# Gate and norm products in three split parts, a new order of the key and value groups, and a new order of the first transfers, in a two-layer decoder trunk

## The chip, the cores and the metric

The kernel is one program for one core of a Trainium2 chip. The metric is the device time of one execution in microseconds (us), as the median of several runs; smaller is better. TensorE (PE in the rows) multiplies, VectorE (DVE), ScalarE (ACT) and GpSimd (POOL) work on elements, SyncE (SP) only starts transfers. ACT and POOL start transfers too, from their own streams of instructions.

## The reference

512 positions of width 1024 pass through two layers. The first is a gated linear recurrence, the second is attention over three groups of dilated windows, and each is followed by a SwiGLU block:

```
h = h + recurrent_mixer(rms_norm(h))      # layer 1
h = h + swiglu(rms_norm(h))
k, v = shared_kv(h)                       # 3 groups x 2 heads of keys and values
h = h + dilated_attention_mixer(rms_norm(h), k, v)    # 3 groups x 8 heads of queries
h = h + swiglu(rms_norm(h))
```

The part that the change touches most is the recurrent mixer:

```
y, x = split(h @ w_in)                    # 1024 -> 2 x 1024
xc = causal_depthwise_conv(x, 4 taps) + b
r, i = sigmoid(xc @ w_a + b_a), sigmoid(xc @ w_x + b_x)     # 8 blocks of 128 x 128
log_a = -8 * r * softplus(-lambda);  a = exp(log_a)
u = sqrt(1 - exp(2 log_a)) * (i * xc)
hr = scan(a, u)                           # h_t = a_t h_(t-1) + u_t
out = (gelu(y) * hr) @ w_out
```

## The kernel before, in words

Everything lies transposed on the chip: 128 features on the partitions, 512 positions in a row, so h is eight tiles of 128x512. A wide product is made of 128x128 weight tiles against 128x512 tiles of activations. Almost all products run in three parts (`mm3`, L146 to L148): weight and activation are each split into a high part of type float32r and the float32r rest (`wh`, `wl`, `xh`, `xl`), and high x high, high x low and low x high are added up in PSUM. Two sorts of product do not run so: the two gates of the recurrence (L388, L389), whose weights `gw` and activations `xc` are plain float32, and the row of norm factors that `norm_rows` (L260 to L265) spreads over all partitions with a matrix of ones (L263).

Weights stream in as pieces of 128x1024 through the class `Stream`: `_load` (L85) asks for a piece, as a rule on SP's queue; two raw pieces (`wr`) are held at a time. `_split` makes the parts: `wh` is a cast on ACT (L100); `wl` is a difference on DVE (L107), or, for pieces marked "dma", a negated copy on ACT (L103) onto which a transfer from POOL's queue adds the original (L104). The first two pieces come in three cuts each (256, 256 and 512 columns), their first cuts on ACT's queue.

The recurrence works by eight blocks of 128 features. `x_block` takes a block out of PSUM and multiplies by the norm row `rb` (`xp`, L377), then runs the four taps of the convolution: the first on ACT (L380), three on DVE (L382), which give `xc`. `x_gates` multiplies `xc` by the two gate weights, two blocks at a time, with sigmoids and a tanh on ACT (L395 to L398) behind. `decays` has the exponentials and square roots on ACT, `recur` the scan on DVE. These steps stand between the blocks of `w_in` (`in_block`), which are 24 matmuls each.

Keys and values (`project`, `done_kv`) run over three groups in the order 0, 1, 2. The values of group 1 are moved between partitions by 16 small transfers on POOL's queue (L755). Queries follow. In the attention itself (`attend`) PE goes through 32 units of scores (`scores`), transposes of the softmax (`turned`, L876) and value products (`values`); between them it is given filling: the projection of later queries (`project_q`, L710 to L712) and the first half of the output projection. Query heads are turned by PE (L789) into a PSUM bank "X" of which there is one, and copied out by ACT (L791). What is due later is put in a list by tick (`at`), which `tick` works off.

The order on each engine comes from a scheduler that follows the order of the program, apart from what stands in `tc.high_priority()` and what `behind` holds back.

## Time and profile before

| | us |
|---|---|
| median of 3 runs | 1215.19 (1214.24 to 1215.32) |
| the profiled execution | 1216.08 |
| its span on the chip | 1214.3 |
| PE busy in it | 1203.3 |
| DVE busy | 659.4 |
| ACT busy | 519.0 |
| POOL busy | 160.7 |

A row of the timeline gives the start and the length of one instruction, or of several alike in a row (xN), and in brackets how long its engine stood idle before and what it waited for. Lengths of matmuls overlap, since they are pipelined: what one costs is read from start to start. A plain float32 matmul leaves two records in the trace.

### The profile page before, as it was taken

To read this page: it belongs to the slowest core of one execution; us is meant where nothing else is said; L and a number is where in the kernel's file an instruction comes from. 1 tells how busy PE (TensorE), PEld (TensorE's weight loads), DVE (VectorE), ACT (ScalarE), POOL (GpSimd) and SP (SyncE) were. 2 spreads that over 40 slices of the span, in tenths; PEclk is the share of its full clock that TensorE was granted. 3 is DMA by queue.
4 is the path that set the end of the run, shared out by engine and by line. 5 is a ranking of instruction groups with operands and counts; after the bars stand their busy time and mean duration, and the time that the engine had idled before them with its cause. 6 is when DMAs were issued, how large, how long until landed. Compare 5 with 4: busy or idle time off the path is not lost.

```text
span 1214.3 us, 14690 instructions
## 1 busy us (share of the span) xinstructions
PE 1203.3 (99%) x5627; PEld 994.8 (82%) x5627; DVE 659.4 (54%) x1232; ACT 519.0 (43%) x751; POOL 160.7 (13%) x163
## 2 busy tenths in 40 slices
PE   9999999999999999999999999999999999999998
PEld 6778888888888888888788888898888888888887
DVE  8787675455454333377555667856545455542221
ACT  6795433323232222265555778655323223222110
POOL 0100001011110000010411344350011011110000
PEclk9999999999999999999999999999999999999999
DMA  7543332332223333323978688535223323233331
GB/s 247 137 104 104 113 109 93 104 97 95 92 99 100 95 96 96 100 97 95 221 173 181 157 177 203 130 71 139 87 93 99 104 90 101 89 98 113 114 116 43
DMA packets 42053, 141.81 MB, mean 117 GB/s; under 512 B 5248, under 2 KB 6144, under 8 KB 41984
## 3 DMA queue, kind: packets, MB, share of 16 engines
q1 hardware_dynamic: 33552, 113.97, 29.6%
q0 software_dynamic: 7280, 25.69, 12.0%
q10 hardware_dynamic: 1152, 1.23, 0.4%
q8 instruction: 44, 0.72, 0.2%
q14 instruction: 25, 0.20, 0.0%
HBM read 137.72 MB, written 2.10 MB: 115 GB/s over the span
## 4 chain that ended last, share of the span: by engine, by line
PE 92%; DVE 2%; DMA 2%; ACT 2%; issue 1%; POOL 1%; ACTq 0%; DVEq 0%; POOLq 0%
PE ps L147 26%; PE ps L148 25%; PE ps L146 25%; PE ps L710 4%; PE ps L711 4%; PE ps L712 4%; DMA wl<-in_w_q 2%; PE ps L789 1%; PE ps L876 1%; PE ps L388 1%; PE ps L389 1%; DVE ql L232 0%; ACT wl L103 0%; PE ps L248 0%; DVE sqc L647 0%
## 5 line engine op out<-in xcount | busy, mean ns | idle before, releaser
L100 ACT CAST wh<-wr 128x1024 fp32r<-128x1024 f32 (+3 forms) x216 | 219.4, 1016 | 480.0 <-PE ps L147 438.3
L146 PE MATMUL ps<-xh,wh 128*128 128x512 f32 x896 | 353.0, 394 | 0.2 <-ACT xh L226 0.2
L147 PE MATMUL ps<-xl,wh 128*128 128x512 f32 x896 | 349.2, 390 | 0.2 <-DVE xl L232 0.2
L148 PE MATMUL ps<-xh,wl 128*128 128x512 f32 x896 | 349.0, 389 | 0.0
L107 DVE TENSOR_TENSOR wl<-wr,wh 128x1024 fp32r<-128x1024 f32 (+2 forms) x169 | 241.0, 1427 | 147.2 <-ACT wh L100 147.1
L146 PEld LDWEIGHTS ps<-xh,wh 128*128 128x128 f32 x896 | 168.4, 188 | 37.0 <-issue 1.2
L147 PEld LDWEIGHTS ps<-xl,wh 128*128 128x128 f32 x896 | 168.3, 188 | 36.7 <-issue 1.7
L148 PEld LDWEIGHTS ps<-xh,wl 128*128 128x128 f32 x896 | 168.2, 188 | 34.8
L148 PE MATMUL ps<-gh,wl 128*128 128x512 f32 x352 | 136.9, 389 | 0.0
L147 PE MATMUL ps<-gl,wh 128*128 128x512 f32 x352 | 136.9, 389 | 0.0
L146 PE MATMUL ps<-gh,wh 128*128 128x512 f32 x352 | 136.9, 389 | 0.0
L493 POOL TENSOR_TENSOR u<-u,g 128x512 f32<-128x512 f32 x44 | 58.8, 1335 | 503.4 <-ACT wh L100 354.2
L492 DVE TENSOR_TENSOR u<-ps,rb 128x512 f32<-128x512 f32 x44 | 30.4, 691 | 135.6 <-PE ps L148 135.6
L710 PE MATMUL ps<-wh,xh 128*128 128x512 f32 x224 | 91.4, 408 | 0.0
L711 PE MATMUL ps<-wl,xh 128*128 128x512 f32 x224 | 87.8, 392 | 2.4 <-DMA wl<-in_w_q 2.4
L712 PE MATMUL ps<-wh,xl 128*128 128x512 f32 x224 | 87.7, 392 | 0.0
L148 PEld LDWEIGHTS ps<-gh,wl 128*128 128x128 f32 x352 | 66.1, 188 | 13.8
L146 PEld LDWEIGHTS ps<-gh,wh 128*128 128x128 f32 x352 | 66.1, 188 | 13.7
L147 PEld LDWEIGHTS ps<-gl,wh 128*128 128x128 f32 x352 | 66.1, 188 | 13.5
L490 DVE TENSOR_TENSOR g<-ps,rb 128x512 f32<-128x512 f32 x44 | 30.4, 691 | 63.7 <-PE ps L148 63.6
L103 ACT ACTIVATE wl<-wr 128x1024 fp32r<-128x1024 f32 x47 | 49.7, 1058 | 24.2 <-PE ps L711 24.1
L231 ACT CAST gh<-u 128x512 fp32r<-128x512 f32 x44 | 27.4, 622 | 60.8 <-POOL u L493 60.8
(214 smaller groups left out, 1459.0 us busy)
## 6 DMA issues: line engine op xcount, KB each, us to landing
wr<-in_f_in SPq DMA_DIRECT2D x88, 512.0 KB, 3.5
wr<-in_f_out SPq DMA_DIRECT2D x32, 512.0 KB, 3.6
wr<-in_w_q SPq DMA_DIRECT2D x32, 512.0 KB, 7.1
wl<-in_w_q POOLq DMA_DIRECT2D x32, 512.0 KB, 7.6
wr<-in_w_in SPq DMA_DIRECT2D x14, 512.0 KB, 3.9
wr<-in_f_out SPq DMA_DIRECT2D x16, 384.0 KB, 3.1
wr<-in_w_kv SPq DMA_DIRECT2D x12, 512.0 KB, 3.4
wr<-in_a_out SPq DMA_DIRECT2D x8, 512.0 KB, 3.4
```

The source lines that it names most:

```text
L100: nc.scalar.copy(hi[:, c], r[:, c])
L103: nc.scalar.mul(lo[:, c], r[:, c], -1.0)
L107: a = eng.tensor_tensor(lo[:, c], r[:, c], hi[:, c].bitcast(F32), ALU.subtract)
L146: PE.matmul(ps, wh, xh, start=first, stop=False)
L147: PE.matmul(ps, wh, xl, start=False, stop=False)
L148: PE.matmul(ps, wl, xh, start=False, stop=last)
L490: V.tensor_tensor(g, pair[0], rb, ALU.mult)
L492: V.tensor_tensor(u, pair[1], rb, ALU.mult)
L493: G.tensor_tensor(u, u, g, ALU.mult)
L710: PE.matmul(ps[t], xh[k][:, r], wh[:, c], start=k == 0, stop=False)
L711: PE.matmul(ps[t], xh[k][:, r], wl[:, c], start=False, stop=False)
L712: PE.matmul(ps[t], xl[k][:, r], wh[:, c], start=False, stop=k == 7)
```

## The change

- **Gates.** Gate weights are split like the others (`gwh`, `gwl`), from a raw piece that is cast and negated on ACT and added onto by a transfer of POOL's. `xc` is split by `x_parts` (high part by a cast on ACT, low part by a difference on DVE), and the gates run as `mm3`. The first tap of blocks 4 to 7 goes to POOL.
- **Norm rows.** `norm_rows` makes a high and a low diagonal (eight DVE operations where there were four) and multiplies both by ones in float32r.
- **Keys and values.** The groups come in the order 0, 2, 1 (the first, the third and the second), and their weights too.
- **Attention.** A unit has one place for filling where it had two, and the turns of the later queries (`kv` = 1) lie two ticks apart where they lay one apart.
- **Start.** The first tile of x is the first transfer of SP; the parameters go to ACT's queue. The second piece of weights comes by SP alone, its first cast waits for the first `xh`, two of nine warm-up matmuls go, and the first two weight blocks alternate by two feature tiles.

The diff, cut to its core:

```diff
@@ Stream._load, Stream._split
+                itertools.zip_longest(self._cuts(i, w), self.queues[i] if i < self.cut else (), fillvalue=self.nc.sync)]
...
+                a = nc.scalar.copy(hi[:, c], r[:, c])
+                if i in self.cast:
+                    behind(self.tc, a, self.cast.pop(i))
@@ the start
-    p_kv = add_pieces([A["w_kv"][i] for i in range(12)])
+    p_kv = add_pieces([A["w_kv"][i] for g in (0, 2, 1) for i in range(4 * g, 4 * g + 4)])
...
-        load_a, load_b, load_c, *splits = ws.start(2, nc.scalar)
-        nc.sync.dma_start(par, A["par"])
-        run(load_a)
+        load_a, load_b, load_c, *splits = ws.start(2, (nc.scalar,), ())
+        nc.scalar.dma_start(par, A["par"])
+        run(load_a[:1])
         for k in range(KB):
             nc.sync.dma_start(h[k], A["x"][k])
-            run({1: load_b, 3: load_c}.get(k, ()))
+            run({0: load_a[1:], 1: load_b, 3: load_c}.get(k, ()))
+        G.tensor_copy(ones_r, ones)
@@ norm_rows
-                a = V.tensor_scalar(dg[:, 128 * n:128 * n + 128], ident, r[:, n:n + 1], None, ALU.mult)
+                c = slice(128 * n, 128 * n + 128)
+                V.tensor_scalar(dh[:, c], ident, r[:, n:n + 1], None, ALU.mult)
+                a = V.scalar_tensor_tensor(dl[:, c], ident, r[:, n:n + 1], dh[:, c].bitcast(F32),
+                                           ALU.mult, ALU.subtract)
...
-            PE.matmul(ps, ones, dg, start=True, stop=True)
+            PE.matmul(ps, ones_r, dh, start=True, stop=False)
+            PE.matmul(ps, ones_r, dl, start=False, stop=True)
@@ the recurrence
-            for _ in range(9):
+            for _ in range(7):
...
+                    else:
+                        ws.cast[1] = a
...
-            for k in range(KB):
-                c = slice(128 * k, 128 * k + 128)
+            for k2 in range(0, KB, 2):
                 for ps, (wh, wl) in zip(first, parts):
-                    mm3(ps, (wh[:, c], wl[:, c]), (xh[k], xl[k]), k == 0, k == KB - 1)
-            gw = [lp.tile([128, 1024], F32, name=f"gw{i}", bufs=1) for i in range(2)]
-            for g in range(2):
-                nc.sync.dma_start(gw[g], A["gates"][g])
+                    for k in (k2, k2 + 1):
+                        c = slice(128 * k, 128 * k + 128)
+                        mm3(ps, (wh[:, c], wl[:, c]), (xh[k], xl[k]), k == 0, k == KB - 1)
...
+            for g in range(2):
+                raw = lp.tile([128, 1024], F32, name="gwr", tag="rate", bufs=4)
+                nc.sync.dma_start(raw, A["gates"][g])
+                S.copy(gwh[g], raw)
+                S.mul(gwl[g], raw, -1.0)
+                nc.gpsimd.dma_start(gwl[g], A["gates"][g], accum_op=ALU.add)
@@ x_block, x_parts, x_gates
-                S.activation(xc, xp[:, 0:T], AF.Identity, bias=gain(C_CB, b), scale=cw[0])
+                if b < 4:
+                    S.activation(xc, xp[:, 0:T], AF.Identity, bias=gain(C_CB, b), scale=cw[0])
+                else:
+                    G.tensor_scalar(xc, xp[:, 0:T], cw[0], gain(C_CB, b), ALU.mult, ALU.add)
...
+            def x_parts(b, xc):
+                parts = [lp.tile([128, T], F32R, name=n) for n in ("xch", "xcl")]
+                halve(xc, *parts)
+                return b, xc, parts
...
-                PE.matmul(pr, gw[0][:, c], xc, start=True, stop=True)
-                PE.matmul(pi, gw[1][:, c], xc, start=True, stop=True)
+                for g, ps in enumerate((pr, pi)):
+                    mm3(ps, (gwh[g][:, c], gwl[g][:, c]), parts, True, True)
...
+                if i in (4, 5, 7, 8):
+                    xs[:2] = [x_parts(*x) for x in xs[:2]]
@@ attention
-            at(lag + j, lambda t=t: turn(t, kn[t]))
+            at(lag + apart * j, lambda t=t: turn(t, kn[t]))
...
-    for g in range(3):
+    for j, g in enumerate((0, 2, 1)):
...
-                    normed(st, 4, 0, turn, {3: 11, 4: 7}.get(j, 8), tiles)
+                    normed(st, 4, 0, turn, {3: 11, 4: 7}.get(j, 8), tiles, 1 + kv)
...
             if u >= LAG:
                 turned(*units[u - LAG])
-            yield u + 0.4
             if u < 32:
                 scores(*units[u])
             yield u + 1.0
...
-        if k % 2:
-            tick()
+        tick()
```

How instructions move is shown at three places. The first is DVE ahead of the first group of gates (blocks 0 and 1), from the `xp` of blocks 2 and 3 on. Before:

```order
L377 TENSOR_TENSOR xp_423<-ps_234,rb_314 128x4x4x32
L377 TENSOR_TENSOR xp_431<-ps_282,rb_314 128x4x4x32
L382 SCALAR_TENSOR_TENSOR xc_426<-xp_423,par_74,xc_426 128x512
L382 SCALAR_TENSOR_TENSOR xc_434<-xp_431,par_74,xc_434 128x512
L382 SCALAR_TENSOR_TENSOR xc_426<-xp_423,par_74,xc_426 128x512
L382 SCALAR_TENSOR_TENSOR xc_434<-xp_431,par_74,xc_434 128x512
L107 TENSOR_TENSOR wl7_456<-wr7_448,wh7_455 128x1024
```

and now, where `xcl_456` and `xcl_460` are the low parts of blocks 0 and 1, and `xc_450` is block 4, whose first tap is POOL's:

```order
L397 TENSOR_TENSOR xp_439<-ps_278,rb_316 128x4x4x32
L237 TENSOR_TENSOR xcl_456<-xc_418,xch_455 128x512
L405 SCALAR_TENSOR_TENSOR xc_434<-xp_431,par_74,xc_434 128x512
L405 SCALAR_TENSOR_TENSOR xc_442<-xp_439,par_74,xc_442 128x512
L405 SCALAR_TENSOR_TENSOR xc_434<-xp_431,par_74,xc_434 128x512
L110 TENSOR_TENSOR wl7_472<-wr7_464,wh7_471 128x1024
L405 SCALAR_TENSOR_TENSOR xc_434<-xp_431,par_74,xc_434 128x512
L405 SCALAR_TENSOR_TENSOR xc_442<-xp_439,par_74,xc_442 128x512
L397 TENSOR_TENSOR xp_447<-ps_324,rb_316 128x4x4x32
L405 SCALAR_TENSOR_TENSOR xc_442<-xp_439,par_74,xc_442 128x512
L405 SCALAR_TENSOR_TENSOR xc_450<-xp_447,par_74,xc_450 128x512
L237 TENSOR_TENSOR xcl_460<-xc_426,xch_459 128x512
```

The low part of block 1 stands behind seven taps, the `wl` of a weight piece and an `xp`, though its own `xc_426` is finished before the first of these rows.

The second place is POOL's queue where the values are moved. Before, transfers of query weights (`wl` from `in_w_q`) stand ahead of, between and behind the moves, of which this is a piece:

```order
L755 DMA vh_3697<-ph 64x2x128
L755 DMA vh_3696<-ph 64x2x128
L104 DMA wl_4486<-in_w_q 128x1024
L755 DMA vh_3697<-ph 64x2x128
L755 DMA vl_3698<-pl 64x2x128
L755 DMA vl_3699<-pl 64x2x128
```

and now, at the end of the moves:

```order
L787 DMA vl_3785<-pl 64x2x128
L787 DMA vl_3784<-pl 64x2x128
L787 DMA vl_3785<-pl 64x2x128
L107 DMA wl_4342<-in_w_q 128x1024
L107 DMA wl_4401<-in_w_q 128x1024
```

All 16 moves now stand ahead of the first transfer of query weights.

The third place is PE in the attention, between two turns of query heads (`ident,kn`). Before, with value products (`ph`, `pl`) and transposes of the softmax (`ident,pr`) between them:

```order
L789 MATMUL ps<-ident,kn 128x128 x4
L146 MATMUL ps<-ph,vh_3696 128x256
L147 MATMUL ps<-pl,vh_3696 128x256
L148 MATMUL ps<-ph,vl_3698 128x256
L146 MATMUL ps<-ph,vh_3696 128x128
L147 MATMUL ps<-pl,vh_3696 128x128
L148 MATMUL ps<-ph,vl_3698 128x128
L146 MATMUL ps<-ph,vh_3696 128x128
L147 MATMUL ps<-pl,vh_3696 128x128
L148 MATMUL ps<-ph,vl_3698 128x128
L876 MATMUL ps<-ident,pr 128x128 x3
L789 MATMUL ps<-ident,kn 128x128 x4
```

and now, at two turns of another unit, with filling between them (`wh`, `wl` against `xh`, `xl`):

```order
L821 MATMUL ps<-ident,kn 128x128 x4
L741 MATMUL ps<-wh_5566,xh 128x512
L742 MATMUL ps<-wl_5567,xh 128x512
L743 MATMUL ps<-wh_5566,xl 128x512
L741 MATMUL ps<-wh_5566,xh 128x512
L742 MATMUL ps<-wl_5567,xh 128x512
L743 MATMUL ps<-wh_5566,xl 128x512
L821 MATMUL ps<-ident,kn 128x128 x4
```

Two turns that follow each other closely now have six matmuls of filling between them.

## Rows read from the trace of the kernel before

**Rows 1.** The page, part 1: engine, busy us, share of the span, instructions.
```profile
PE 1203.3 (99%) x5627; PEld 994.8 (82%) x5627; DVE 659.4 (54%) x1232; ACT 519.0 (43%) x751; POOL 160.7 (13%) x163
```

**Rows 2.** The page, part 2: granted TensorE clock in 40 slices.
```profile
PEclk9999999999999999999999999999999999999999
```

**Rows 3.** The page, part 4: the chain that ended last, by engine.
```profile
PE 92%; DVE 2%; DMA 2%; ACT 2%; issue 1%; POOL 1%; ACTq 0%; DVEq 0%; POOLq 0%
```

**Rows 4.** Timeline of PE around the first group of gates.
```profile
39.13 0.39 PE L147 MATMUL ps<-xl,wh 128*128 128x512 f32 x1
...
40.95 1.02 PE L388 MATMUL ps<-xc,gw 128*128 128x512 f32 x2
...
44.61 0.40 PE L147 MATMUL ps<-xl,wh 128*128 128x512 f32 x1
```

**Rows 5.** Groups of PE by form: count of records, busy us, mean ns, idle before.
```profile
L388 PE MATMUL ps<-xc,gw 128*128 128x512 f32 x16 | 8.2, 591 | 0.0
L389 PE MATMUL ps<-xc,gw 128*128 128x512 f32 x16 | 8.2, 592 | 0.0
L263 PE MATMUL ps<-dg,ones 128*128 128x512 f32 x6 | 3.1, 590 | 0.0
```

**Rows 6.** Timeline of PE at the start: the first product.
```profile
5.65 0.97 PE L146 MATMUL ps<-xh,wh 128*128 128x512 f32 x2 [0.19 <-ACT xh L226]
```

**Rows 7.** Timeline of ACT at the start.
```profile
4.57 0.40 ACT L100 CAST wh<-wr 128x256 fp32r<-128x256 f32 x1 [0.88 <-DMA wr<-in_w_in]
4.88 0.72 ACT L226 ACTIVATE xh<-h,par 128x512 fp32r<-128x512 f32 x1
```

**Rows 8.** Timeline of DVE ahead of the first gates.
```profile
23.48 0.87 DVE L260 TENSOR_SCALAR dg<-ident,nry 128x128 f32<-128x128 f32 x4
...
26.14 0.69 DVE L265 COPY rb<-ps 128x512 f32<-128x512 f32 x1 [0.27 <-PE ps L263]
...
29.04 4.21 DVE L382 SCALAR_TENSOR_TENSOR xc<-xp,par,xc 128x512 f32<-128x512 f32 x6
33.16 1.99 DVE L377 TENSOR_TENSOR xp<-ps,rb 128x512 f32<-128x512 f32 x2
...
38.09 1.22 DVE L107 TENSOR_TENSOR wl<-wr,wh 128x1024 fp32r<-128x1024 f32 x1
```

**Rows 9.** Timeline of DVE in the first SwiGLU.
```profile
242.65 2.33 DVE L107 TENSOR_TENSOR wl<-wr,wh 128x1024 fp32r<-128x1024 f32 x1 [0.21 <-ACT wh L100]
244.89 0.68 DVE L232 TENSOR_TENSOR gl<-u,gh 128x512 fp32r<-128x512 f32 x1
```

**Rows 10.** Timeline of POOL at the same time.
```profile
242.60 1.28 POOL L493 TENSOR_TENSOR u<-u,g 128x512 f32<-128x512 f32 x1 [9.59 <-ACT wh L100]
```

**Rows 11.** Groups of POOL by form: the softmax's scaling.
```profile
L864 POOL TENSOR_SCALAR pr<-pr,den 128x512 f32<-128x512 f32 x16 | 26.0, 1626 | 26.6 <-DVE den L863 25.4 <-PE ps L876 1.2
```

**Rows 12.** Timeline of ACT in the recurrence.
```profile
61.63 2.01 ACT L410 ACTIVATE tau<-tau 128x1024 f32<-128x1024 f32 x2
...
65.89 1.05 ACT L103 ACTIVATE wl<-wr 128x1024 fp32r<-128x1024 f32 x1
```

**Rows 13.** Timeline of PE at the first query weights.
```profile
605.82 0.39 PE L710 MATMUL ps<-wh,xh 128*128 128x512 f32 x1
607.72 0.50 PE L711 MATMUL ps<-wl,xh 128*128 128x512 f32 x1 [1.51 <-DMA wl<-in_w_q]
```

**Rows 14.** The chain that ended last, in order of time, there: start, us, work.
```profile
597.28 0.58 POOL vl L755
597.86 9.82 DMA wl<-in_w_q
```

**Rows 15.** Timeline of PE in the attention: three waits.
```profile
700.50 0.66 PE L789 MATMUL ps<-ident,kn 128*128 128x128 f32 x4 [0.73 <-ACT qt L791]
...
718.88 0.66 PE L789 MATMUL ps<-ident,kn 128*128 128x128 f32 x4 [0.53 <-ACT qt L791]
...
759.75 0.50 PE L711 MATMUL ps<-wl,xh 128*128 128x512 f32 x1 [0.86 <-DMA wl<-in_w_q]
```

More of the change, by code (lines that the diff above doesn't have):

```diff
@@ L78, in __init__ @@
         self.hold = {}
+        self.cast = {}
     def _load(self, i):
@@ L99, in do @@
             with self.tc.high_priority():
-                nc.scalar.copy(hi[:, c], r[:, c])
+                a = nc.scalar.copy(hi[:, c], r[:, c])
+                if i in self.cast:
+                    behind(self.tc, a, self.cast.pop(i))
                 kind = self.pieces[i][1]
@@ L191, in trunk @@
         ones = kp.tile([128, 128], F32, name="ones")
+        ones_r = kp.tile([128, 128], F32R, name="ones_r")
         ssum = kp.tile([128, T], F32, name="ssum")
@@ L254, in norm_factors, with norm_rows @@
             return mean_squares(pool, [ssum[:, 128 * n:128 * n + 128] for n in range(4)], "nr")[1]
-        def norm_rows(pool, r, tag="sq", bufs=1, copy=S.copy, hold=None):
-            dg = pool.tile([128, T], F32, name="dg", tag=tag, bufs=bufs)
+        def norm_rows(pool, r, tag="sq", bufs=1, copy=S.copy, hold=None, low=None):
+            dh, dl = (pool.tile([128, T], F32R, name=n, tag=g, bufs=b)
+                      for n, g, b in (("dgh", tag, bufs), ("dgl", *(low or ("dgl", 1)))))
             ps = bank("O")
             for n in range(4):
-                a = V.tensor_scalar(dg[:, 128 * n:128 * n + 128], ident, r[:, n:n + 1], None, ALU.mult)
+                c = slice(128 * n, 128 * n + 128)
+                V.tensor_scalar(dh[:, c], ident, r[:, n:n + 1], None, ALU.mult)
+                a = V.scalar_tensor_tensor(dl[:, c], ident, r[:, n:n + 1], dh[:, c].bitcast(F32),
+                                           ALU.mult, ALU.subtract)
             if hold:
                 ws.hold[hold] = a
-            PE.matmul(ps, ones, dg, start=True, stop=True)
+            PE.matmul(ps, ones_r, dh, start=True, stop=False)
+            PE.matmul(ps, ones_r, dl, start=False, stop=True)
             rb = pool.tile([128, T], F32, name="rb", bufs=1)
@@ L327, in trunk @@
             first.append(in_block(2, between=lambda: soon(norm_factors, small)))
-            first.append(in_block(3, between=lambda: soon(norm_rows, lp, norm[0], "q", 3, V.tensor_copy, 4)))
+            first.append(in_block(3, between=lambda: soon(norm_rows, lp, norm[0], "q", 3, V.tensor_copy, 4, ("q", 3))))
             rb = norm[1]
             first.append(in_block(4, "PT"))
+            gwh, gwl = ([lp.tile([128, 1024], F32R, name=f"{n}{i}", bufs=1) for i in range(2)] for n in ("gwh", "gwl"))
+            for g in range(2):
[4 more added lines that the diff above has]
+                nc.gpsimd.dma_start(gwl[g], A["gates"][g], accum_op=ALU.add)
             lam = par[:, C_LAM:C_LAM + 8]
@@ L360, in trunk @@
             hgh = [lp.tile([128, T], F32R, name=f"hgh{k}", bufs=1) for k in range(KB)]
-            hgl = [lp.tile([128, T], F32R, name=f"hgl{k}", bufs=1) for k in range(KB)]
+            hgl = [None] * KB
             gated = [lp.tile([128, T], F32, name=f"gated{k}", bufs=1) for k in range(KB)]
@@ L429, in y_gate @@
                 V.tensor_tensor(z, z, gated[b], ALU.mult)
+                hgl[b] = lp.tile([128, T], F32R, name="hgl", tag=f"gated{b}", bufs=1)
                 halve(z, hgh[b], hgl[b])
@@ L438, in trunk @@
                     for _ in range(2):
-                        b, xc = xs.pop(0)
-                        x_gates(b, xc)
+                        b = xs[0][0]
+                        x_gates(*xs.pop(0))
                     if b % 4 == 3:
@@ L659, in rotate, with normed @@
         V.tensor_tensor(x[:, :, 0:32], a, b, ALU.add)
-    def normed(st, nh, tab, turn, lag, tiles=range(4)):
+    def normed(st, nh, tab, turn, lag, tiles=range(4), apart=1):
         kn = dict(zip(tiles, st["kn"]))
@@ L768, in done_kv @@
                 normed(st, 2, tab, turn, 10)
-        for _ in project(p_kv + 4 * g, *((xh, xl) if g == 0 else (xph, xpl)), done_kv):
+        for _ in project(p_kv + 4 * j, *((xh, xl) if g == 0 else (xph, xpl)), done_kv):
             pass
```

3 lines of the change are left out of this document (1 added, 2 removed).

## The prediction

> **What bounds the kernel now.** I read the page first, then the timelines of the places that the change touches. PE is busy for 1203.3 of 1214.3 us [rows 1], its clock is granted in full (2.4 GHz) in all 40 slices [rows 2], and 92% of the chain that ended last is PE's own work [rows 3]. So time comes out of this kernel in two ways only: fewer PE microseconds, or fewer waits of PE, and any new wait of PE costs its full length. DVE is busy for 54% over the whole span [rows 1], but ahead of the first gates its rows follow each other with next to no gap [rows 8], so there an added DVE operation counts.
>
> **Gates.** Start to start, eight split matmuls take 40.95 - 39.13 = 1.82 us, 0.2275 each [rows 4]. From 40.95 to 44.61 lie four gate matmuls and one split one [rows 4]: (3.66 - 0.23) / 4 = 0.858 us for a gate matmul. There are 32 records, two to a matmul, so 16 matmuls [rows 5]. In three parts each costs 0.683, 0.175 less: **-2.8 us**. The Trainium skill (FP8 and Floating Point Precision, TensorE Precision Notes) says that true FP32 takes four passes; by that and the 0.2275 a gate would cost 0.91 and the change would save 3.6 here, and the whole sum would be about 1 us better. The row shows less than four passes' worth, 3.8, and the row is used.
>
> **Norm rows.** Six records are three matmuls, of the same length as the gates' [rows 5]. Two parts of 0.2275 for 0.858 save 0.40 each: **-1.2 us**. The four added low diagonals on DVE are costed below for the first stage; in the two SwiGLU stages a block of 24 matmuls (5.5 us) hides them, and if it did not they would cost 4 x 0.22 = 0.9 us each [rows 8].
>
> **Start.** The first product begins at 5.65 and waits for the first `xh` [rows 6], which began at 4.88 behind a cast that had itself waited 0.88 for a transfer of weights [rows 7]. Now `xh` stands ahead of that cast and its tile is asked for first. Nothing shows how soon both can be there: the gain lies between 0 (the weights decide as before) and 0.9. Against it, the gate weights now put four passes of about 1.0 us [rows 12] on ACT in the first stage, ahead of the third and fourth weight pieces; a late piece would cost up to one of them. I take **-0.3**, bounds -0.9 and +0.8. Two warm-ups fewer cost nothing while PE waits for data; should the first products start at the lower of the clock's two levels (1.2 GHz), each would take twice its 0.2275, and the bound of +0.8 holds three of them.
>
> **Keys and values.** At 605.82 PE starts a matmul, and the next begins at 607.72, idle 1.51 and 1.67 late, for a piece of query weights [rows 13]. The chain follows it back: that transfer was issued at 597.86, right behind the value moves on POOL's queue, and took 9.82 us [rows 14]. Now all 16 moves stand ahead of all query weights, so this wait goes: **-1.6**, bounds 0 (another piece is late instead) and -1.7. What is late next would be the first pieces of query weights, issued behind the last move; the third group now ends with the values that move, but its norms and turns still stand between those moves and the first query product.
>
> **Attention.** The filling is the same work in other portions, and the distances between transposes, scores and values add up alike. Three waits of PE are seen in rows: 0.73 and 0.53 for ACT's copy out of bank X, and 0.86 for a piece of weights [rows 15]. The piece's negated copy now comes ahead of its cast on ACT, which frees about 1.0 us [rows 12], so that the 0.86 goes. The turns have new spacing: pairs of them have six matmuls of filling, 1.4 us, in between, where the wait of 0.73 arose with value products and transposes of about the same length in between. I take **-0.8**; bounds -2.1 (all three go) and +3.1 (six close pairs at 0.73 each, less the two that are there).
>
> **The new wait.** The gates now need a high and a low part of `xc`. Both come late in DVE's order: `xcl` of block 1 stands behind work for blocks 2, 3 and 4. `rb` began at 26.14 [rows 8]; four low diagonals at 0.22 come ahead of it, less the 0.27 that it waited, so it starts at 26.8. Behind it: itself 0.6, two `xp` 2.0, six taps 4.1, two `xp` 2.0, `xcl` of block 0 0.7 [rows 9], three taps 2.1, a `wl` 1.15, two taps 1.4, an `xp` 1.0, a tap 0.7 [rows 8], together 15.75, to 42.5. The next tap, of block 4, needs POOL's first tap, which can begin when its `xp` ends at 41.8 and takes 1.63 if it runs like the nearest POOL operation of this size [rows 11]: 43.4. Then a tap and the `xcl`: 44.8. PE comes to that product at 40.95 - 0.4 (norm row) - 0.3 (start) + 8 x 0.23 = 42.1. So PE waits 2.7; with no POOL delay 1.8; with DVE held up by POOL, as below, 3.4. I take 3.0. All of PE's blocks stand behind it. The second group gains slack from that wait. The third and fourth have ACT's `xch` behind the square roots (2.01) and behind a cast and a negated copy (1.05) [rows 12], about when PE comes: between nothing and one `xcl` of 0.68 for each of four blocks, 2.7; I take 1.0. Together **+4.0**, bounds 1.0 and 6.1, the latter without any further contention.
>
> **The sum.** -2.8 - 1.2 - 0.3 - 1.6 - 0.8 + 4.0 = -2.7 us. The profiled execution of 1216.08 would become 1213.4. It lies 0.9 above the median of the runs, 1215.19, so the median becomes **1212.5**.
>
> **Rivals.**
>
> *DVE keeps up.* If the scalar chain behind `sp` fills gaps that I count as work, or POOL's tap is quick, the gates wait 1.0 in all. For: DVE had small idle gaps there, such as the 0.27 [rows 8]. Against: the order on DVE is fixed and its sum is 1.8 over even without POOL. -2.7 - 3.0 = -5.7: 1209.5. Chance 0.20.
>
> *POOL holds DVE up: slower.* Beside POOL's `u` of 1.28 us [rows 10], DVE's `wl` took 2.33 us [rows 9], where it takes 1.22 alone [rows 8]: 1.1 longer. The first taps of blocks 4 to 7 now run on POOL beside taps, low parts and gated products on DVE, in the stage where DVE sets the pace. Four times 1.1 is 4.4 on top, and DVE's delay would reach PE at the gates; with the attention's 0.8 not gained either, -2.7 + 4.4 + 0.8 = +2.5: 1217.7. It decides from about 9.1 us of waits at the gates (8.3 if the attention gives nothing). Against: some of that DVE work has slack, above all once PE has waited at the first group. Chance 0.17. The Trainium skill (SBUF — State Buffer, Who interferes with whom) has a rule for this: a DVE instruction with two inputs in SBUF and a GpSimd instruction that reads SBUF exclude each other, and whichever starts first blocks the other for its whole length. By that rule, the trace agrees: 2.33 against 1.22.
>
> *The turns collide.* The close pairs of turns wait for the single bank X as the one at 700.50 does [rows 15]: +3.1 in place of -0.8, so -2.7 + 3.9 = +1.2: 1216.4. For: the same distance has produced a wait. Against: that wait came from ACT being busy, not from the distance. Chance 0.13.
>
> *The new key order does not do what it says.* The moves, ahead of the weights now, delay the first pieces as much as they delayed the later ones: -2.7 + 1.6 = -1.1: 1214.1. For: one such transfer took 9.82 us when the moves were under way [rows 14]. Chance 0.08.
>
> **How the numbers follow.** My forecast has 0.42. A measurement of this kernel can tell about 0.2%, 2.4 us, from no change, so faster means below 1212.8 and slower above 1217.6. The forecast lies near the first bound: 0.22 of its 0.42 is faster, 0.20 the same. With the rivals (all of the first; 0.12 of the second slower and 0.05 the same; of the third 0.09 the same, 0.03 slower, 0.01 faster; of the fourth 0.06 the same, 0.02 faster) that makes faster 0.45, same 0.40, slower 0.15. The range runs from a little below the first rival, 1208.5, to the second, 1217.7. The forecast's own range, from its bounds taken half each way, is 1210 to 1215.
>
> **What would show it.** In the timeline of PE after, the 16 gates appear as 48 records 0.23 apart, with an idle of about 3 us before the `xcl` of block 1 at some 42 us, put down to DVE. If that idle is under 1 us, the first rival holds. POOL's first taps should take some 1.6 us each; if DVE rows beside them show more than 1 us extra and PE idles at all four groups, the second holds. The three norm rows cost two records each. The first product should start between 4.7 and 5.7. Around 600 us no wait of PE for query weights should be left, and in the attention no turn should wait over 0.7 us for ACT. I am wrong about the sum if PE's busy time has not fallen by about 4 us, and about the waits if its idle has not grown.

## The result, and the profile after

The changed kernel takes **1221.31 us** (median of four executions, 1219.96 to 1223.16) where the one before takes 1215.26 in the same comparison: a ratio of 1.0046, with an interval of 1.0034 to 1.0059. It is slower by about 6 us, where 2.7 us less had been forecast. The profiled execution (1221.2 us, span 1219.4) lies in the middle of the four; where the other three lost their time isn't shown.

PE's busy time and the chain that ended last, from the page of the changed kernel:

```profile
PE 1202.2 (99%) x5641; PEld 999.0 (82%) x5641; DVE 665.2 (55%) x1252; ACT 524.5 (43%) x759; POOL 168.3 (14%) x170
PE 89%; DVE 5%; ACT 3%; issue 2%; DMA 2%; POOL 0%; DVEq 0%; ACTq 0%; POOLq 0%
```

PE's busy time fell by 1.1 us only [rows 1], where about 4 had been forecast, and its share of the chain by three points [rows 3]. Where the time went is read by landmarks: the start of the same matmul in both timelines of PE, stretch by stretch (the products are counted from 0; the last stretch ends at the last matmul).

| stretch | before | after | difference |
|---|---|---|---|
| to the 100th product of `w_in` (its norm row saves 0.43) | 30.97 | 32.28 | +1.31 |
| from there to the 140th | 9.07 | 13.56 | +4.49 |
| from there to the recurrence's output projection (all the gates) | 69.09 | 69.28 | +0.19 |
| from there to the first turn of queries (SwiGLU, keys and values) | 440.27 | 439.84 | -0.43 |
| from there to the first transpose of the softmax | 130.92 | 128.95 | -1.97 |
| from the first to the last transpose (attention) | 140.28 | 142.33 | +2.05 |
| the rest | 389.24 | 388.76 | -0.48 |

So norm rows (three times 0.4) and the key order paid as forecast; the first 46 us and the attention lost far more. The start in the timeline of PE:

```profile
1.44 3.17 PE L300 MATMUL ps<-warm 128*128 128x512 bf16 x7 [1.44 <-DVE warm L297]
5.84 0.80 PE L149 MATMUL ps<-xh,wh 128*128 128x512 f32 x1 [1.23 <-ACT wh L101]
...
9.19 0.63 PE L150 MATMUL ps<-xl,wh 128*128 128x512 f32 x1
9.62 0.63 PE L151 MATMUL ps<-xh,wl 128*128 128x512 f32 x1
10.04 0.57 PE L149 MATMUL ps<-xh,wh 128*128 128x512 f32 x1
10.45 0.40 PE L150 MATMUL ps<-xl,wh 128*128 128x512 f32 x1
10.69 0.40 PE L151 MATMUL ps<-xh,wl 128*128 128x512 f32 x1
```

The first product comes 0.19 later than before [rows 6]. From 7.1 to 10.0 the products follow each other 0.43 apart, as the warm-ups do (the first two distances are 0.6), and from 10.5 on 0.23; before, the second product already began that pace, at 6.2. Why no product comes sooner: the first `xh` needs the parameters, which now land at 4.46 (3.10 before), and an exponential stands ahead of it on ACT. So it begins at 4.79, only 0.09 sooner than before [rows 7], and the cast of the weights, which now stands behind it, is what the product waits for. From the timeline of ACT:

```profile
4.68 0.21 ACT L358 ACTIVATE l<-l 128x8 f32<-128x8 f32 x1 [1.75 <-DVE l L357]
4.79 0.71 ACT L231 ACTIVATE xh<-h,par 128x512 fp32r<-128x512 f32 x1
5.41 0.39 ACT L101 CAST wh<-wr 128x256 fp32r<-128x256 f32 x1
...
31.07 1.05 ACT L101 CAST wh<-wr 128x1024 fp32r<-128x1024 f32 x1 [7.30 <-DMA wr<-in_w_in]
```

The last of these rows belongs to the second loss. The sixth weight piece comes late, its transfer onto the negated copy starts late, and PE stands still for it. PE's timeline there, and the same stretch by windows (start:end, length, busy time and count of PE, PEld, DVE, ACT, POOL, then the granted clock, the DMA engines' share and GB/s):

```profile
37.04 0.39 PE L150 MATMUL ps<-xl,wh 128*128 128x512 f32 x1
40.01 0.50 PE L151 MATMUL ps<-xh,wl 128*128 128x512 f32 x1 [2.58 <-DMA wl<-in_w_in]
...
41.81 0.63 PE L151 MATMUL ps<-xh,wl 128*128 128x512 f32 x1
42.23 0.63 PE L149 MATMUL ps<-xh,wh 128*128 128x512 f32 x1
```

```profile
37.00:41.00 4.00, 1.42 (x6) 0.86 (x6) 4.00 (x7) 3.13 (x5) 0.77 (x3) 1.00 1.00 257
41.00:45.00 4.00, 4.00 (x12) 3.08 (x11) 4.00 (x6) 0.67 (x1) 0.10 (x1) 0.57 0.68 130
45.00:60.00 15.00, 14.59 (x65) 11.66 (x64) 11.68 (x17) 13.04 (x19) 5.15 (x8) 1.00 0.50 134
```

PE idles 2.58 us, and behind the idle stretch the granted clock is 0.57 over four microseconds, with products 0.43 apart: the lower of the two levels. Start to start the wait cost 2.74, which leaves 1.75 of the 4.49 for the low clock.

The waits of PE in the whole recurrence, summed by what ended them (total, times, longest):

```profile
PE ps L151 <- DMA wl<-in_w_in: 2.6, 1, 2.6
PE ps L150 <- DVE xcl L237: 1.6, 3, 0.7
PE ps L300 <- DVE warm L297: 1.4, 1, 1.4
PE ps L149 <- ACT wh L101: 1.2, 1, 1.2
```

and in the attention (680 to 830 us):

```profile
PE ps L821 <- ACT qt L823: 2.2, 4, 0.8
PE ps L150 <- DVE xl L237: 1.2, 1, 1.2
PE ps L149 <- DVE mn L889: 1.0, 1, 1.0
PE ps L741 <- DVE sqc L678: 1.0, 1, 1.0
PE ps L150 <- DVE pl L237: 0.4, 2, 0.2
PE ps L151 <- DVE ql L237: 0.2, 1, 0.2
```

The wait of 0.86 for query weights [rows 15] is gone, but turns wait four times for ACT's copies, and there are new waits for the softmax maximum (`mn`), the norm chain (`sqc`) and a split (`xl`).

### The profile page after: what moved, and what is told of

It reads as the page before. It is cut to its first block, busy times and chain, and to the rows that moved or that the text cites. A ratio compares the mean times of both kernels' runs of the same rounds, so it can differ in the third digit from the quotient of the medians.

```text
span 1219.4 us, 14746 instructions
## 1 busy us (share of the span) xinstructions
PE 1202.2 (99%) x5641; PEld 999.0 (82%) x5641; DVE 665.2 (55%) x1252; ACT 524.5 (43%) x759; POOL 168.3 (14%) x170
## 4 chain that ended last, share of the span: by engine, by line
PE 89%; DVE 5%; ACT 3%; issue 2%; DMA 2%; POOL 0%; DVEq 0%; ACTq 0%; POOLq 0%
PE ps L150 25%; PE ps L151 25%; PE ps L149 24%; PE ps L741 5%; PE ps L742 4%; PE ps L743 4%; DMA wr<-in_w_o 1%; PE ps L821 1%; ACT wl L106 1%; ACT pr L894 1%; DMA wl<-in_w_in 1%; ACT wh L101 1%; PE ps L908 0%; DVE ql L237 0%; DVE pl L237 0%
## 5 line engine op out<-in xcount | busy, mean ns | idle before, releaser
L896 POOL TENSOR_SCALAR pr<-pr,den 128x512 f32<-128x512 f32 (+2 forms) x32 | 45.2, 1412 | 62.2 <-DVE den L895 55.8
```

The lines of the kernel that those rows point to most:

```text
L896: G.tensor_scalar(pr[:, :width], pr[:, :width], den, None, ALU.mult)
```

## The experiments

The times of the table are medians. The kernel before was timed in each comparison on the same chip; its median differed from chip to chip (1215.26 to 1217.51), so ratios compare better than microseconds. The last seven rows come from two chips on which single executions of the kernel before reached 1223 us, so a small difference between their ratios and those of the rows above shows nothing. Each run has one profile, and a run's median holds more than the effect of its edit (the waits at 37 and at 760 us come and go, as shown below), so an edit is judged by the landmarks of its own stretch.

| run | us | ratio to before | interval |
|---|---|---|---|
| the change | 1221.31 | 1.0046 | 1.0034 to 1.0059 |
| nine warm-ups | 1220.27 | 1.0044 | 1.0029 to 1.0059 |
| gate low part by POOL | 1225.34 | 1.0080 | 1.0065 to 1.0095 |
| gates plain again | 1217.28 | 1.0011 | 1.0000 to 1.0021 |
| attention as before | 1218.55 | 1.0023 | 1.0012 to 1.0034 |
| start as before | 1217.40 | 1.0016 | 1.0005 to 1.0028 |
| parameters first | 1218.68 | 1.0022 | 1.0013 to 1.0031 |
| turns as before | 1220.32 | 1.0040 | 1.0025 to 1.0055 |
| norm rows and key order alone | 1214.05 | 0.9993 | 0.9983 to 1.0003 |
| gate transfers held behind | 1219.24 | 1.0009 | 0.9995 to 1.0022 |
| norm rows, key order and gates | 1219.16 | 1.0010 | 0.9996 to 1.0024 |
| the same, parts early | 1215.71 | 0.9987 | 0.9971 to 1.0003 |
| norm rows, key order, turns | 1214.84 | 0.9977 | 0.9963 to 0.9992 |
| no gate transfers | 1220.19 | 1.0012 | 0.9994 to 1.0030 |
| nine warm-ups, transfers behind | 1219.42 | 1.0001 | 0.9983 to 1.0018 |
| parts early, no gate transfers | 1214.25 | 0.9960 | 0.9944 to 0.9977 |

**Nine warm-ups.**

```diff
-            for _ in range(7):
+            for _ in range(9):
```

> The changed kernel with nine warm-up matmuls instead of seven, nothing else. Theory A (clock): in the changed kernel PE stood idle for 1.23 us behind its seven warm-ups, its first eleven products then ran 0.43 apart instead of 0.23; nine warm-ups leave a gap as short as before (0.2 us), so the products run 0.23 apart from about 6.8 on, the norm row comes at about 25.5 instead of 27.75, and the time falls by about 2.2 us, to about 1219. Rival (data): the early products are slow because splits of weights and x come late; then the first dozen products keep their distances and the time stays within 0.5 us of 1221.3.

The products ran 0.23 apart from 8.1 on (10.5 with the change) and the fifteenth came at 10.35 (11.61): the direction of theory A, though it expected 6.8. But the fiftieth came at 18.98 (19.54), because PE then waited 0.41 for the third piece's `wl`, and the hundredth at 32.11 (32.28). The low rate is real, but what is gained there is lost again a little later, and the ratio, 1.0044 against 1.0046, shows no gain.

**The gate weights' low part by POOL.**

```diff
-                S.mul(gwl[g], raw, -1.0)
-                nc.gpsimd.dma_start(gwl[g], A["gates"][g], accum_op=ALU.add)
+                G.tensor_tensor(gwl[g], raw, gwh[g].bitcast(F32), ALU.subtract)
```

> The changed kernel, but the low part of the gate weights is a difference made by POOL from the raw piece; the two negated copies on ACT and the two transfers of 512 KB that add onto them go. Theory B (transfers): those two transfers, issued at 21.3 and 23.2, share the DMA engines with the sixth-block weight piece asked for at about 22, which took 8.8 us instead of some 4, and so PE stood idle 2.6 us at 40.0 for that block's low part; without them the piece lands 3 to 4 us sooner, the idle at 40 goes, the clock does not fall behind it (another 1.9 us), and the time falls by about 4 us, to about 1217. Rival (ACT): the wait comes from the gate weights' four passes on ACT and from the pieces being asked for later; two passes fewer then move it by at most 1 us, and the time stays above 1220. A second rival (shared port): POOL's two operations hold up DVE's splits of the weights at 17 to 25 us, and the time does not fall.

The second rival came true. POOL's timeline, and then DVE's:

```profile
16.00 2.86 POOL L348 TENSOR_TENSOR gwl<-gwr,gwh 128x1024 fp32r<-128x1024 f32 x1 [14.28 <-ACT gwh L347]
20.39 2.68 POOL L348 TENSOR_TENSOR gwl<-gwr,gwh 128x1024 fp32r<-128x1024 f32 x1 [1.53 <-ACT gwh L347]
```

```profile
14.90 0.17 DVE L364 TENSOR_TENSOR l<-l,l 128x8 f32<-128x8 f32 x1
...
16.50 2.38 DVE L364 TENSOR_TENSOR l<-l,l 128x8 f32<-128x8 f32 x1
...
18.99 1.23 DVE L110 TENSOR_TENSOR wl<-wr,wh 128x1024 fp32r<-128x1024 f32 x1
...
20.74 2.36 DVE L364 TENSOR_TENSOR l<-l,l 128x8 f32<-128x8 f32 x1
...
23.21 0.68 DVE L245 TENSOR_TENSOR ssum<-ssum,sq 128x512 f32<-128x512 f32 x1
```

DVE's operations with two inputs stop while POOL's run: the small operation `l`, which takes 0.17 alone, takes 2.38 and 2.36 and ends at 18.88 and 23.10, where POOL's operations end at 18.86 and 23.07. The operations behind it start at 18.99 and 23.21, and PE waited 1.59 and 2.20 for them. This is the rule of the Trainium skill (SBUF — State Buffer, Who interferes with whom) that such a DVE instruction and a GpSimd instruction that reads SBUF exclude each other for their whole length; the trace agrees. The sixth weight piece landed 3.8 us after it was asked for (8.8 with the change) and PE did not wait for it; but it came there five microseconds later, so this run alone does not show what the transfers cost.

**Gates as before.**

```diff
-                    mm3(ps, (gwh[g][:, c], gwl[g][:, c]), parts, True, True)
+                    PE.matmul(ps, gw[g][:, c], xc, start=True, stop=True)
```

with `gw` loaded whole, no parts, and all first taps on ACT.

> The changed kernel with the gates as before: plain float32 weights and activations, no parts, all first taps on ACT; norm rows, start, key order and attention stay changed. Theory: the gates' change as a whole costs the 2.74 + 1.9 us at 40 to 45 us and 2.4 us of waits in front of the low parts, and saves 2.8 us of PE; undone, the time falls by about 4.2 us, to about 1217. Rival (clock or start only): the loss is in the start and the attention, and undoing the gates costs 2.8 us: about 1224.

1217.28. No wait at 37 us and none at the gates; PE reached the output projection 1.47 us behind the kernel before (5.99 with the change). The 1.47 are there by the hundredth product (32.44): the start. From there to the output projection plain gates take as long as before (78.16 us), and the gates as changed 4.7 longer in the changed kernel's profile, 1.4 to 2.7 longer in those of seven other kernels here that keep gates and gate transfers. The difference is the wait at 37 us, which is 2.6 in the first, with the low clock behind it, and 0.9 or less in the seven, without.

**Attention as before, and the turns alone.** The first undoes filling and spacing, the second the spacing only:

```diff
+            yield u + 0.4
             if u < 32:
                 scores(*units[u])
...
-        tick()
+        if k % 2:
+            tick()
...
-            at(lag + apart * j, lambda t=t: turn(t, kn[t]))
+            at(lag + j, lambda t=t: turn(t, kn[t]))
```

> The changed kernel with the attention's filling as before (two places for filling in a unit, ticks as before, turns one tick apart). Theory D: from the first to the last transpose of the softmax PE took 2.05 us more than before; the new filling is the reason, and undone the time falls by about 2 us, to 1219.3, with the waits at 717.6 (softmax maximum) and 757.1 gone. Rival: the longer stretch comes from the state in which the attention is entered (the key order and the earlier first unit), so the waits move but stay in sum, and the time stays within 0.7 us of 1221.3.

> The changed kernel with the turns of the later queries one tick apart as before, the filling in one piece as changed. Theory D: the filling in one piece moves the cost (the waits for the softmax maximum at 717.6 and for the norm chain at 757.1 come from the scores that stand closer to what they wait for); the time stays within 0.7 us of 1221.3 and the stretch of the softmax's transposes stays 2 to 3 us longer than before. Rival: the spacing of the turns is what costs (waits of PE for ACT's copies at 706, 722, 745 and 772, 2.8 us in sum); one tick apart they go and the time falls by 2 us or more.

With the attention as before the stretch of transposes took 140.5 us, against 140.3 before and 142.3 with the change. With the old spacing alone it took 145.0. With the attention as before the waits for `mn` and `sqc` are gone, as theory D has it. Waits with the old spacing alone, and a window of its clock:

```profile
PE ps L821 <- ACT qt L823: 2.9, 4, 1.3
PE ps L741 <- DVE sqc L678: 1.9, 1, 1.9
PE ps L150 <- DVE xl L237: 1.2, 1, 1.2
PE ps L149 <- DVE mn L889: 0.9, 1, 0.9
```

```profile
779.00:782.00 3.00, 3.00 (x10) 2.52 (x11) 2.95 (x14) 0.60 (x2) 0.80 (x1) 0.50 0.96 254
```

Over all profiles, the ten with the filling in one piece take 142.1 to 145.3 us for the stretch (middle 143.2). Of the seven with the filling in two places, the one before among them, six take 139.8 to 141.9 (middle 140.4) and the last (parts early, no gate transfers) 143.8. Part of this is the clock. In seven of the ten, and in the last of the seven, the granted clock falls to its lower level between 755 and 783 us, at waits of PE of 1.2 to 2.2 us; waits of up to 1.5 us passed without a fall in others, the changed kernel among them. An estimate: half of the time at the lower level, 1.7 us in each of the seven and 3.4 in the last, is what it costs. Without it the ten take 140.7 to 143.6 (middle 142.0) and the seven 139.8 to 141.9 (middle 140.4). So the filling costs about 1.6 us in waits, and in most of these executions another 1.7 by the clock. What the spacing does beside it can't be told: with the filling in one piece the changed spacing reaches from 140.7 to 143.6 without the low clock, and the old one, with 143.3, lies among them.

**The start as before, and the parameters alone.** The first puts back order, queues, warm-ups and alternation of the start; the second only this:

```diff
-        nc.scalar.dma_start(par, A["par"])
+        nc.sync.dma_start(par, A["par"])
```

> The changed kernel with the whole start as before: parameters first on SP, first cuts of both weight pieces on ACT's queue, first cast not held behind the first xh, nine warm-ups, blocks alternating by one feature tile. Norm rows, gates, key order and attention stay changed. Theory E: the new start costs about 1.6 us (the hundredth product came 1.3 us later than before although the norm row saves 0.4), because parameters on ACT's queue land at 3.9 to 4.5 instead of 3.1 and because the scalar chain behind them, with an exponential on ACT ahead of the first xh, stands in front of x; undone, the hundredth product comes at about 30.6 and the time falls by 1.6 us against the first runs of this start, to about 1219. Rival: the squares and the gate weights' passes on ACT and DVE at 15 to 22 us set the pace there whatever the start; the hundredth product then stays at 32 and the time stays above 1220.5.

> The changed kernel with only the parameters put back to the head of SP's queue (the first tile of x second). Theory E: the parameters' transfer on ACT's queue (3.7 us to landing, 2.4 before) is what holds the first xh; on SP's queue they land at about 3.1, the first product starts at about 4.9 instead of 5.3 to 5.8, and the hundredth comes 0.4 to 0.8 us sooner, for about 1220.5. Rival: the first product then waits for its weights, whose first cut comes on ACT's queue; it starts no sooner than 5.3 and the time is the changed kernel's.

With the whole start undone the hundredth product came at 31.49, 0.8 sooner. That is 0.7 behind the kernel with norm rows and key order alone (30.82, below), and 0.6 of it is there by the fifteenth; in this profile the second `xh` was late behind a cast that had waited 0.74 for a cut of weights. With the parameters first the first product started at 4.86, a microsecond sooner, the products ran at the low rate until 10, and the hundredth came at 32.06, 0.2 sooner. The first product does not set the pace. The executions of both gained more than that, 1.0016 and 1.0022 against 1.0046, which neither theory nor rival of the parameters' run has. In both profiles the sixth weight piece took 4.3 us in place of 8.8, and PE waited 0.75 and 0 for it; whether the order of the start does that is open, as the runs without gate transfers show.

**Gate weights behind the weight pieces, and that with nine warm-ups.**

```diff
-                nc.sync.dma_start(raw, A["gates"][g])
+                behind(tc, nc.sync.dma_start(raw, A["gates"][g]), ws.loads[3])
```

> The changed kernel with the two transfers of gate weights held behind the third and fourth weight pieces on SP's queue. Theory F: in the new start the first gate piece of 512 KB goes out at 7.7, ahead of the third weight piece (10.9), which therefore lands and is cast 2 us later than before (16.4 against 14.1); that, and not the first product, is what the start costs. Held behind, the cast comes at about 15 and the hundredth product at about 31.5 instead of 32.1 to 32.3, so about 0.7 us are gained. Rival (first products): the start's cost is the late parameters and the slow first products alone; the hundredth product stays at 32.1 or later. Gate weights that come later could also delay the first gates; then the gain is lost again by 43 us.

> The changed kernel with nine warm-ups and with the gate weights' transfers behind the third and fourth weight pieces. Theories A and F together: each alone gained little because either of the two delays (first products at the low rate until 9 to 11 us; third piece cast 2 us late) is hidden by the other. With both undone the fifteenth product comes at about 10.3 (11.6 in the changed kernel), the fiftieth at 18.3 (19.5) and the hundredth at 31.1 to 31.3 (32.2), and the time falls by about 1 us. Rival: something else in the first stage, such as DVE's chain of squares or late tiles of x, sets the hundredth product; it stays at 32.

Alone, the hundredth product stayed at 32.20: the third piece came in time, but the products ran at the low rate until 10.8. With both, the fifteenth came at 9.65, the fiftieth at 17.59 and the hundredth at 30.82, just where the kernel with norm rows alone has it. By these landmarks theories A and F hold together, and neither alone: two delays of about equal size lay side by side. They rest on one profile each; the executions, 1219.24 and 1219.42 on two chips, can't show the expected gain of 1 us. In the eight profiles with seven warm-ups the products reached 0.23 apart at 8 to 11 us (in one at 8.0, in the rest from 9.0 on), in the nine with nine warm-ups by 9.1 at the latest.

**Norm rows and key order alone, and with the spacing of the turns.** The kernel before with these parts of the change, and then:

```diff
-            at(lag + j, lambda t=t: turn(t, kn[t]))
+            at(lag + apart * j, lambda t=t: turn(t, kn[t]))
```

> The kernel before with two parts of the change alone: norm rows in two split parts, and the key groups in the order first, third, second. Start, gates and attention as before. Theory: these are the two parts that pay; three norm rows save 0.43 each and the wait of 1.67 for query weights at 606 goes, together about 2.9 us, so 1212.3 against 1215.2 to 1215.7. Rival: the weights' wait comes back in the old attention, or the norm row's longer DVE chain delays the first stage (its copy waited 1.1 us for PE in the changed kernel); then the time is within 0.8 us of the kernel before.

> The kernel before with norm rows, key order, and of the attention's change the spacing of the later turns alone (two ticks apart), the filling in two places as before. Theory D: the filling in one piece is what costs in the attention (with it and the old spacing the stretch of transposes was 4.7 us longer than before, with it and the new spacing 2.0 to 3.3), and the spacing takes off 1.5 us or so; with the old filling it removes the waits for ACT's copies at 698.0, 716.4 and 778.3 (2.3 us in sum), so the time is 1 to 2 us under that of the run with norm rows and key order alone. Rival: the spacing only helps where the filling stands in one piece; the stretch then stays within 0.7 us of that run's 140.3 us.

By landmarks the first saves 2.94 us against the profile of the kernel before; by executions 0.07%, with an interval that just holds 1. With the turns two ticks apart the stretch of transposes is 139.8 us (140.3), no turn waits for ACT any more, and its waits are

```profile
PE ps L718 <- DMA wl<-in_w_q: 1.0, 2, 0.6
PE ps L148 <- DVE ql L234: 0.5, 1, 0.5
PE ps L146 <- ACT qt L798: 0.4, 1, 0.4
```

The gain is 0.5 where 1 to 2 were expected: waits for weights grow as those for the copies go, and the stretch stays within the rival's 0.7. At 0.9977 (0.9963 to 0.9992) this is the one kernel here that computes the whole result and has its interval below 1.

**The gates on that base, and with their parts early.** The second calls for the parts in high priority and has all first taps on ACT:

```diff
-                    xs[:2] = [x_parts(*x) for x in xs[:2]]
+                    with tc.high_priority():
+                        xs[:2] = [x_parts(*x) for x in xs[:2]]
```

> The kernel before with norm rows, key order and the gates in split parts (first taps of the later blocks on POOL), but with start and attention as before; it differs from the run with norm rows and key order by the gates alone. Theory B: the gates save 2.8 us of PE and cost more in waits: about 0.8 for a weight piece's low part at 37 us, about 3.4 for low parts of xc at the four groups, 0.7 by ACT's four passes ahead of the weight pieces; so PE reaches the output projection of the recurrence 2 to 3 us later than without them, and the time is 1216.3 to 1217. Rival: with the old start DVE and ACT come in time, the waits shrink under 2.8 us and the time is 1213 or less.

> The same as the run with the gates alone, but the split of xc into its parts is put ahead of later work in the scheduler's order (on DVE both low parts of the first group come right behind their taps), and all first taps are on ACT. Theory B: the wait at the first group (about 1.2 us) goes, and those at the third and fourth groups (1.9 us together) shrink at least by half, so the gates about break even with plain float32 ones: 1213.5 to 1215. Rival (weights): work put ahead on ACT and DVE delays the weight pieces by as much, PE waits for those instead, and the time is the one of the run with the gates alone.

In both profiles PE waited for the sixth piece, 3.0 and 3.4 us, and the low clock came with it; PE reached the output projection 5.6 and 4.4 us later than with norm rows and key order alone, where 2 to 3 and about nothing had been expected. Parts early removed the waits at the first three groups (1.0 is left at the fourth). The executions of the second lie in two groups: seven of 1214.5 to 1215.8 at a granted clock of 1.000, five of 1218.1 to 1219.3 at 0.997 to 0.999.

**No transfers of gate weights.**

```diff
-                S.mul(gwl[g], raw, -1.0)
-                nc.gpsimd.dma_start(gwl[g], A["gates"][g], accum_op=ALU.add)
+                S.mul(gwl[g], raw, 0.0)
```

> The changed kernel without the two transfers that add the gate weights onto their negated copies; the low part of the gate weights is written as zero by the same two passes on ACT, so this part of the product is left out of the result while every engine does the same work. Theory B (transfers): PE's wait for a low part at 37 to 40 us (0.6 to 3.4 us in the profiles with these transfers) goes, the sixth piece lands about 4 us after it is asked for instead of 8.8, no low clock follows at 41 to 45, and the time falls by 1 to 4 us. Rival (ACT and order): the piece is late because of ACT's passes and of its late request; the wait stays at 0.5 us or more.

> The run with the gates' parts put early, without the two transfers that add onto the gate weights (low part of the gate weights zero, left out of the result). Theory B: that run's executions fall in two groups, 1214.5 to 1215.8 at full clock and 1218.1 to 1219.3 at 0.997 to 0.999, because the weight piece at 36 us is late by a varying amount and the clock falls when PE idles long; without the transfers the second group goes, and the executions lie at 1213 to 1215.5 on a chip where the kernel before takes 1215.3. Rival: the two groups come from elsewhere (the start); the spread stays.

The second of these also has the turns two ticks apart, which its expectation does not say; it differs from the run it names by that as well. In the first, the sixth piece was cast at 25.58, 5.5 us sooner, as ACT's timeline shows:

```profile
25.58 1.05 ACT L101 CAST wh<-wr 128x1024 fp32r<-128x1024 f32 x1 [1.94 <-DMA wr<-in_w_in]
26.54 1.05 ACT L106 ACTIVATE wl<-wr 128x1024 fp32r<-128x1024 f32 x1
```

PE passed 37 to 40 us without a wait and without a low clock. What the transfers of weight pieces took, beside and without those of the gates, is seen here (asked for from 21.0 to 23.9 us; the changed kernel, then this run):

```profile
gwl<-in_gates POOLq DMA_DIRECT2D x2, 512.0 KB, 8.2
wr<-in_w_in SPq DMA_DIRECT2D x1, 512.0 KB, 8.8
```

```profile
wr<-in_w_in SPq DMA_DIRECT2D x1, 512.0 KB, 3.4
```

Of the weight pieces asked for between 18 and 40 us the slowest took 5.4 us. The ratio is 1.0012 against 1.0046, though on this chip the executions scatter widely, and there a kernel that keeps the transfers (nine warm-ups, transfers behind) had 1.0001: a gain in executions is not shown.

The wait at the first group's low part came out at 1.97 then, close to the 2.7 of the forecast: in the changed kernel the earlier wait for the piece had hidden it. So the stretch from the hundredth product to the output projection still takes 2.1 us longer than before. And the transfers do not make the piece late in every execution. Over all profiles the sixth piece takes 4.1 to 8.8 us in the ten of kernels that keep them, and 3.4 to 3.8 in the seven others, the one before among them. Of the ten, three have the wait (2.6 to 3.4 us) and a low clock with it; seven wait 0.9 or less there and have none. Two of the ten are of kernels that are the same up to the attention (start as before; norm rows, key order and gates): the piece took 4.3 us in one and 8.2 in the other.

In the run with parts early and no gate transfers PE reached the output projection at 109.42, as early as with plain gates (109.13 before; 113.40 with the transfers), and the ratio is 0.9960; its spread did not go (three of ten executions at 0.997, 1216.4 to 1217.4), so not every low clock comes from this wait; in its profile the clock falls at 758 us, at a wait of 1.70 for query weights. A way to make the low part without these transfers and without DVE's or POOL's time was not found, and moving the transfers behind the sixth piece was not tried.

## Why the prediction was wrong, point by point

By landmarks three terms missed by amounts of the same order, all to the slower side: the gates with their waits came to +4.7 where +1.2 was forecast, the attention to +2.05 (-0.8), the start to +1.7 (-0.3).

- **Norm rows** (-1.2): right, 0.43, 0.43 and 0.48. **Keys and values** (-1.6): right, -1.97; no wait for query weights is left around 600 us.
- **Gates on PE** (-2.8): the matmuls are 48 and 0.23 apart. The saving is there, but it is the smaller part of that item.
- **The new wait** (+4.0) is the step that failed first and by most: it came to 7.5 (4.49 + 0.19, and the 2.8 saved). It looked for late parts of `xc`, and those waits are real: 2.4 us in this profile, 3.7 with nine warm-ups. What the sum left out is that the added transfers compete. It counted the gate weights' passes on ACT, and put the two transfers of 512 KB onto their negated copies at nothing; they run at 21 to 32 us beside the sixth weight piece, and without them that piece comes 5.5 us sooner and the wait is gone. It also took a wait of PE to cost its length, and this one pulled the clock down: 2.58 us of it cost 4.49. Where the piece is not late, as in seven other profiles, the gates came to +1.4 to +2.7, close to the forecast's -2.8 + 4.0, and by the mechanism that it gave (waits for `xcl` of 2.5 to 3.3 us).
- **The start** (-0.3) had the wrong sign: +1.7. The sum took the first product as what counts. It did not follow SP's queue on: the first gate piece goes out ahead of the third weight piece. And it put two warm-ups fewer at nothing and bounded the low rate by three products, where it lasted for ten.
- **The attention** (-0.8): the wait for query weights went as forecast, and the turns collided somewhat (2.2 us where 1.3 were). The step that failed is that the filling is the same work in other portions and adds up alike: in one piece it brings scores, norm chain and split closer to what they need. The bound of +3.1 held the size of the loss, from another cause.
- **The range** took each bound by half. Its upper bounds for start, attention and waits with the other terms as forecast add up to +4.4, and +5.2 is what the profile shows: three errors to the same side, which half bounds leave out.
- **POOL's first taps**, the rival on the slower side: they took 0.8 to 2.0 us, and DVE waited 2.2 us for them in all, but they were not what made it slower. The rival named the right side by the wrong mechanism; what it says of DVE and POOL showed itself in the run with POOL's differences.

## What to carry to other kernels

Follow every transfer that an edit adds down its queue and ask what shares the DMA engines with it in those microseconds: a wait of PE of 2.6 us came from two transfers that nobody waits for until later. One profile shows one execution: the same instructions had a piece landing in 4.3 us or in 8.2. Where PE is the bound, a wait that pulls the clock down costs more than its length, 4.5 us for 2.6 here. When undoing one delay gains nothing, undo it together with its neighbour before giving the theory up.

## What was not expected of the hardware

At the start the products ran 0.43 apart for three microseconds while the profile gives a granted clock of 1.00; there only the distance shows the rate. In the profile with turns as before the clock does read 0.5 there, from 7.5 to 10.9 us. In eleven of the seventeen profiles the clock fell to its lower level in mid-kernel, at waits of PE of 1.2 to 3.4 us, and products ran 0.43 apart. At the sixth weight piece it did so in three profiles though PE had been busy without a gap for over ten microseconds ahead. The page's row of 40 slices shows none of it: in the changed kernel all slices are nines, as before [rows 2].
